# A rewritten opening in a fixed order, and the small products of recurrence and attention issued in larger groups

## The chip, the cores and the metric

One core of a Trainium2 chip runs one decoder layer in one launch. The time is device microseconds of that launch. Matrix products run on TensorE (PE), copies with a scale and functions from a table on ScalarE (ACT), elementwise work on VectorE (DVE), some of it on GpSimd (POOL). Loads are issued from the queue of SyncE (SP), some from POOL's (among them `wdu`, which the first products of the recurrence read, and the positions, `posi`).

## The reference

The sequence has 256 tokens, the model 1024 channels. One projection gives the inputs of two branches, an RWKV-7 recurrence with 8 heads of 64 channels and an attention with 8 heads of 64; each is projected back, gated, and a gated MLP with a short convolution follows.

```python
h = rms_norm(x, norm1_g); proj = h @ w_in            # 1824 + 1536 + 2048 columns
z = z + mu * (shift_right(z) - z)                     # token shift
w_log = -softplus(-(decay_bias + tanh(xw) @ w_decay_up)) - 0.5
a = sigmoid(aaa_bias + xa @ w_aaa_up)
kk = k*k_k / norm(k*k_k);  k = k * (1 + (a - 1) * k_a)
for each token:                                       # state per head 64 x 64
    sa = S @ (-kk_t)
    S  = S * decay_t + sa (x) (kk_t * a_t) + v_t (x) k_t
    y_t = S @ r_t
y_a = (groupnorm(y) + sum(r*k*r_k) * v) * (sigmoid(xg) @ w_gate_up)
y_b = softmax(causal(q k^T / 8)) v                    # q, k normed, partly rotated
x = x + (sigmoid(gate_a) * (y_a @ w_a) + sigmoid(gate_b) * (y_b @ w_b)) @ w_out
u = rms_norm(x, norm2_g) @ w_up                       # halves ua, ub, 2816 columns each
x = x + (gelu(conv3(ua)) * ub) @ w_down
```

With 256 tokens and attention blocks of 256 keys, the choice of blocks leaves each query only its own block, so the attention is plain causal attention.

## The kernel before

**Full products.** The activations stand as a high and a low part (`hh` and `hl`, both in the tile `hx`; `ybh` and `ybl` for the attention's output). Each weight tile is split in the same way: `raw` (512 KB, four buffers) is loaded by SP, its high part `whi` (four buffers) is cast by ACT (L246; three early tiles by DVE), and the remainder `wlo` (three buffers) is taken by DVE (L256). Only when the remainder is done is the next `raw` issued (`load_next`, L234). Three products per tile follow: high by high (L284), low by high (L286) and high by remainder (L289), each 128x128 by 256 columns; for q, k and v of the attention 512 columns (L305, L306, L309). These are the "full products" below. Their sums go to the PSUM pool `acc` (three banks). The small products of the recurrence use the pool `ch` (three banks), those of the attention `at` (two).

**The opening.** x comes in four pieces on SP's queue, then four weight tiles, then ten small parameter loads into `p_100` (L397: shift factors, biases, norm weights), then the fifth weight tile. x is squared and scaled, turned by PE (`xt`, L352), and written as `hx` by ACT (L357) and DVE (L358). DVE also casts the first weight tile, forms its remainder (L256), copies the parameters from PSUM (`late_params`), sets constants (`late_consts`) and computes the angles of the rotation (`rope_tables`). The first three quarters of a projection give `xwa` and `xg`; products on `xwa` (L494) open the recurrence.

**The recurrence** (thread "chain") works on chunks of 64 tokens, four per sequence, eight heads, in products of 64 rows or 64 columns, so on half of the array. In order: `pw` (L494) gives decay and a; `pss` and `prx` (L546) give the norm of k; POOL and DVE write the scaled keys `KB` (POOL's part at L572); `pgr` (L592) multiplies keys by queries inside each chunk, and DVE masks the result into `G` (L595). The 16x16 diagonal blocks of G go through DRAM to `Tb`, where DVE inverts them in 15 steps of two instructions (L612, L614, on `Xb`), and through DRAM again to `X` (L623). `pk`, `pv` and `pz0` prepare the keys, values and right-hand sides. `level()` extends the inverse from 16 to 32 and from 32 to 64 rows (`pp` L704, `px` L714, `py` L720); level(0) serves chunks 0 and 1, level(1), a thread "lv1" of its own, chunks 2 and 3. Then for each chunk `pz` (L772), `pu` (L779), `pS` (L788) and `pyt` (L804, L808); a thread "gn" normalises the results (`pc`, L754).

**The attention** (thread "att") turns q and k (`qkT`), and then takes four blocks (two halves of the tokens, two halves of the heads): scores `ps` (L876), mask, maximum and exponentials (L889) on DVE and ACT, scaling by the sum (four L893), transposes `ppt` (L904), the product with v, `po` (L913), and the split of the output into `ybh` (ACT, L917) and `ybl` (DVE, L918).

**The order.** A thread "bulk" holds the full products: k, r, v of the recurrence, q, k, v of the attention, eight gate products (`gates(1)`, `gates(0)`), and `branch(1)`, the projection of the attention's output, which waits for "att". A loop takes the threads in turn; each yields a cost (PE's time) and a latency after which it may go on:

```python
cost, lat = next(th[1])
now_t += cost
th[2] = now_t + lat * SLACK.get(th[0], 1.0)
```

So what comes out is one order per engine, in which small groups stand between full products. A scheduler places the rest (`tc.issue_after` adds an edge). After the threads come `branch(0)`, the output projection (its result is turned for the MLP, `xt`), and the MLP (L1044, L1047, L1062 to L1064).

Of the kernel before, what the change touches and what calls it, by code (L numbers as in the profile page):

```python
# [11 lines left out]
I32 = mybir.dt.int32  # L12
# [24 lines left out]
def body(tc, x, positions, norm1_g, w_in, rwkv_mu, w_decay_up, decay_bias, w_aaa_up,  # L37
# [5 lines left out]
    with ctx:  # L43
# [6 lines left out]
        HI_ENG = {i: dve for i in (4, 5, 6)}  # L50
# [36 lines left out]

        p0 = t1("p0", (8, 128))
        nc.gpsimd.dma_start(p0, rows(norm1_g, 8))
        x_sb = load_x()  # L90

        ones = cst.tile([128, 512], mybir.dt.bfloat16, name="ones")
        dve.memset(ones, 1.0)

        def keep_warm(n):

            p = acc("idle")
            for _ in range(n):
                pe.matmul(p, ones[:, 0:128], ones, start=True, stop=True)

        keep_warm(8)
        jp = t1("jp", (128, 128), I32)
        pool.iota(jp, pattern=[[1, 128]], base=0, channel_multiplier=-1)
        ident = cst.tile([128, 128], F32, name="ident")
        pool.tensor_scalar(ident, jp, 0.0, None, op0=OP.is_equal)
        eps1 = cst.tile([128, 2], F32, name="eps1")
        dve.memset(eps1[:, 0:1], NORM_EPS)
        dve.memset(eps1[:, 1:2], GN_EPS)
        warm = cst.tile([128, 1], F32, name="warm")
        act.activation(warm, eps1[:, 0:1], AF.Sqrt)  # L110
        jl = t1("jl", (128, 2, 64), I32)
        for q in range(2):
            pool.iota(jl[64 * q:64 * q + 64], pattern=[[0, 2], [1, 64]], base=0,
                      channel_multiplier=-1)
        p1 = t1("p1", (51, 128))
        p1_loads = []
        at = 0
        mu1 = rwkv_mu[0]
        for r, n in ((mu1[0:1792].rearrange("(n c) -> n c", c=128), 14),
                     (mu1[1696:1824].rearrange("(n c) -> n c", c=128), 1),  # L120
                     (rows(decay_bias, 4), 4), (rows(aaa_bias, 4), 4), (rows(k_k, 4), 4),
                     (rows(k_a, 4), 4), (r_k[0].rearrange("h n -> (h n)").rearrange("(n c) -> n c", c=128), 4),
                     (rows(ln_g, 4), 4), (rows(ln_b, 4), 4), (rows(norm2_g, 8), 8)):
            p1_loads.append((p1[at:at + n], r))
            at += n
        assert at == 51
        p2 = t1("p2", (88, 128))

# [8 lines left out]
        def late_consts():  # L137
            dve.tensor_scalar(gmask[:, 0:64], jl[:, 0], 0.0, None, op0=OP.is_gt)
            dve.tensor_scalar(gmask[:, 64:128], jl[:, 1], 0.0, None, op0=OP.is_ge)
            dve.memset(bones, 0.0)  # L140
            for q in range(2):
                dve.memset(bones[64 * q:64 * q + 64, 64 * q:64 * q + 64], 1.0)
            dve.tensor_reduce(rowf, ident.rearrange("p (a b c) -> p a b c", a=4, b=2)[:, :, 1, :],
                              axis=AX.XY, op=OP.add)
            dve.memset(m16, 0.0)
            dve.memset(m32, 0.0)
            for q in range(4):
                o = 32 * (q % 2)
                dve.memset(m16[32 * q:32 * q + 32, o:o + 16], 1.0)
                if q % 2:  # L150
                    dve.memset(m32[32 * q:32 * q + 32, 0:32], 1.0)
            dve.tensor_scalar(m16, m16, rowf, None, op0=OP.mult)
            dve.tensor_scalar(cmask, jp, 0.0, NEG, op0=OP.is_gt, op1=OP.mult)
            dve.memset(rst, 1.0)
            dve.memset(rst.rearrange("p (c i) -> p c i", i=64)[:, :, 0:1], 0.0)

# [3 lines left out]
        pt = atp("pt")  # L160
        pe.transpose(pt[:, 0:8], p0, ident[:8, :8])
        keep_warm(3)
# [21 lines left out]
        def small_loads():  # L184
            nc.gpsimd.dma_start(p2[0:66], conv_w[0].rearrange("w (n c) -> (w n) c", c=128))
            nc.gpsimd.dma_start(p2[66:88], rows(conv_b, 22))

            nc.gpsimd.dma_start(wdu[0:64], w_decay_up[0])
            nc.gpsimd.dma_start(wdu[64:128], w_aaa_up[0])
            nc.gpsimd.dma_start(wgu[:, 0], w_gate_up[0, 0:128])  # L190

            pool.memset(wgu[0:96, 1], 0.0)
            nc.gpsimd.dma_start(wgu[96:128, 1], w_gate_up[0, 128:160])
            for i, g in enumerate((q_norm_g, k_norm_g)):
                nc.gpsimd.dma_start(gqk[:, i], bass.AP(tensor=g.tensor, offset=g.offset,
                                                       ap=[[0, 128], [1, 64]]))
            nc.gpsimd.dma_start(posi, positions[0].rearrange("(t p) -> p t", p=128))

        trig = cst.tile([128, 2, 2, HALF], F32, name="trig")

        def rope_tables():
# [23 lines left out]
            act.activation(trig, ang, AF.Sin)  # L225
# [3 lines left out]
        def load_next():  # L229
            if queue:  # L230
# [3 lines left out]
                nc.sync.dma_start(raw[:, :k * c].rearrange("p (k c) -> p k c", k=k), ap)  # L234
# [4 lines left out]
        def split_hi(eng=None):  # L239
            if raws:  # L240
                eng = eng or HI_ENG.get(nhi[0])
                nhi[0] += 1
                raw, k, c = raws.pop(0)
                hi = wp.tile([128, 1024], F32R, name="whi", tag="whi", bufs=NHI)
                if eng in (None, act):
# [5 lines left out]
        def split_lo():  # L251
            if halves:
# [3 lines left out]
                dve.tensor_tensor(lo[:, :n], raw[:, :n], hi[:, :n].bitcast(F32), op=OP.subtract)  # L256
# [56 lines left out]
        def norm_t(src, g0, tagn, cuts):  # L313
# [40 lines left out]
            def second(mid=lambda a, d: None):  # L354
                for k in range(8):
# [4 lines left out]
                    if k == 3:  # L360
                        mid(a, d)
# [785 lines left out]
```

## Time and profile before

| | us |
|---|---|
| median of 3 runs | 437.18 (437.11 to 437.87) |
| the profiled execution | 437.27 |
| its span in the trace | 435.5 |
| PE busy, share of the span | 424.9, 98% |
| DVE busy | 327.6, 75% |
| ACT busy | 241.9, 56% |
| POOL busy | 12.8, 3% |
| full products with 256 columns: L284, L286, L289 | 64.0 + 62.5 + 40.1 |
| full products with 512 columns: L305, L306, L309 | 20.3 + 18.8 + 15.0 |
| MLP, up: L1044, L1047 | 96.7 + 54.6 |
| MLP, down: L1062 to L1064 | 31.2 each |
| casts of weights on ACT, L246 (121, 1050 ns each) | 126.4 |
| remainders on DVE, L256 (125, 1219 ns each) | 152.0 |

The rows of the trace in the next sections begin with the start in us from the span's start and the busy time in us; then engine, line, operation, what is written from what is read, the shape and the count. A bracket at the end gives the idle time just before the row and what ended it. Matmuls overlap in the array, so the busy times of PE add up to more than passes; the distance from one start to the next tells what a matmul costs. In the page's 40 slices PE is busy for nine tenths or more in all but four (the first two, the seventh and the last), and the granted clock of TensorE is nine tenths or more in all but the second. 70.7 MB move in the span, at 162 GB/s.

### The profile page before, as it was taken

The page shows a single profiled execution, that of the slowest core. Times are in us where ns is not written, and L with a number is a line of the kernel's source. Part 1 is how long each engine was busy: PE and PEld are TensorE (multiplying, and loading weights), DVE is VectorE, ACT ScalarE, POOL GpSimd, SP SyncE. Part 2 cuts the span into 40 slices and gives each one's busy share as a digit, 9 for nine tenths or more (in the row PEclk, how much of TensorE's full clock was granted, in tenths as well). Part 3 has the DMA queues.
Part 4 walks back from the last instruction along what each step waited for, and adds up shares of the span by engine and source line. Part 5 has one row for each costly group of instructions (what it writes and reads, how often), then busy time and mean ns, then how long its engine had stood idle before and what let it go on. Part 6 is the DMA issues. An engine that isn't in the chain of part 4 may idle for free.

```text
span 435.5 us, 8161 instructions
## 1 busy us (share of the span) xinstructions
PE 424.9 (98%) x3248; PEld 367.7 (84%) x3248; DVE 327.6 (75%) x589; ACT 241.9 (56%) x391; POOL 12.8 (3%) x21
## 2 busy tenths in 40 slices
PE   7899998999999999999999999999999999999996
PEld 3789996788899989799997887888888888888885
DVE  4695899698456568676796489797797786786883
ACT  6489852644375446777355377554454564564540
POOL 6000040000000000000000000000000000000000
PEclk9899999999999999999999999999999999999999
DMA  8764836543658331153566365766656556656622
GB/s 232 202 190 124 238 99 195 134 130 52 194 151 233 85 115 53 50 189 116 179 174 192 121 187 161 231 195 197 192 180 208 189 168 211 199 156 212 192 76 96
DMA packets 62187, 70.72 MB, mean 162 GB/s; under 512 B 8898, under 2 KB 52617, under 8 KB 62150
## 3 DMA queue, kind: packets, MB, share of 16 engines
q1 hardware_dynamic: 61750, 69.50, 53.4%
q0 software_dynamic: 400, 0.71, 0.6%
q8 instruction: 25, 0.41, 0.4%
q14 instruction: 12, 0.10, 0.1%
HBM read 68.76 MB, written 1.44 MB: 161 GB/s over the span
## 4 chain that ended last, share of the span: by engine, by line
PE 80%; ACT 6%; DVE 6%; DMA 4%; issue 1%; SPq 1%; DVEq 0%; ACTq 0%
PE acc L1044 17%; PE acc L1047 8%; PE acc L284 6%; PE acc L286 5%; PE acc L289 5%; PE acc L305 4%; PE f L1063 4%; PE f L1062 4%; PE f L1064 4%; PE acc L306 4%; PE acc L309 4%; DMA raw<-in_w_in_dram 3%; DVE wlo L256 2%; ACT whi L246 2%; PE ps L876 1%
## 5 line engine op out<-in xcount | busy, mean ns | idle before, releaser
L246 ACT CAST whi<-raw 128x1024 fp32r<-128x1024 f32 x121 | 126.4, 1050 | 117.5 <-PE acc L1044 46.6
L256 DVE TENSOR_TENSOR wlo<-raw,whi 128x1024 fp32r<-128x1024 f32 x125 | 152.0, 1219 | 45.9 <-PE acc L1047 12.9
L1044 PE MATMUL acc<-hx,whi 128*128 128x512 f32 x352 | 96.7, 395 | 0.6 <-DVE bs L1052 0.6
L1044 PEld LDWEIGHTS acc<-hx,whi 128*128 128x128 f32 x352 | 60.1, 188 | 9.1 <-DVE bs L1052 1.0
L284 PE MATMUL acc<-hx,whi 128*128 128x256 f32 x248 | 64.0, 292 | 0.7 <-ACT whi L246 0.5
L286 PE MATMUL acc<-hx,whi 128*128 128x256 f32 x248 | 62.5, 285 | 0.3 <-DVE hx L358 0.2
L1047 PEld LDWEIGHTS acc<-hx,wlo 128*128 128x128 f32 x352 | 53.4, 188 | 7.9
L1047 PE MATMUL acc<-hx,wlo 128*128 128x256 f32 x352 | 54.6, 278 | 0.0
L284 PEld LDWEIGHTS acc<-hx,whi 128*128 128x128 f32 x248 | 47.4, 191 | 2.9 <-ACT whi L246 0.7
L286 PEld LDWEIGHTS acc<-hx,whi 128*128 128x128 f32 x248 | 47.4, 191 | 1.9 <-DVE hx L358 0.7
L289 PE MATMUL acc<-hx,wlo 128*128 128x256 f32 x248 | 40.1, 285 | 1.0 <-DVE wlo L256 0.9
L289 PEld LDWEIGHTS acc<-hx,wlo 128*128 128x128 f32 x248 | 33.8, 192 | 1.7 <-DVE wlo L256 1.6
L1063 PE MATMUL f<-whi,hb 128*128 128x512 f32 x80 | 31.2, 390 | 0.0
L1064 PE MATMUL f<-wlo,hb 128*128 128x512 f32 x80 | 31.2, 390 | 0.0
L1062 PE MATMUL f<-whi,hb 128*128 128x512 f32 x80 | 31.2, 390 | 0.0
L1052 DVE TENSOR_REDUCE an<-acc 128x256 f32<-128x512 f32 x22 | 15.2, 689 | 7.2 <-PE acc L1047 6.3
L305 PE MATMUL acc<-whi,hx 128*128 128x512 f32 x48 | 20.3, 425 | 0.0
L306 PE MATMUL acc<-whi,hx 128*128 128x512 f32 x48 | 18.8, 392 | 0.0
L1064 PEld LDWEIGHTS f<-wlo,hb 128*128 128x128 f32 x80 | 15.0, 188 | 3.2
L1062 PEld LDWEIGHTS f<-whi,hb 128*128 128x128 f32 x80 | 15.0, 188 | 2.8
L1063 PEld LDWEIGHTS f<-whi,hb 128*128 128x128 f32 x80 | 15.0, 188 | 2.7
L309 PE MATMUL acc<-wlo,hx 128*128 128x512 f32 x48 | 15.0, 393 | 0.0
(280 smaller groups left out, 637.9 us busy)
## 6 DMA issues: line engine op xcount, KB each, us to landing
raw<-in_w_ffn_up_dram SPq DMA_DIRECT2D x44, 512.0 KB
raw<-in_w_in_dram SPq DMA_DIRECT2D x43, 512.0 KB
raw<-in_w_ffn_down_dram SPq DMA_DIRECT2D x22, 512.0 KB
raw<-in_w_out_dram SPq DMA_DIRECT2D x8, 512.0 KB
x<-in_x_dram SPq DMA_DIRECT2D x8, 256.0 KB
raw<-in_w_branch_b_dram SPq DMA_DIRECT2D x4, 512.0 KB
raw<-in_w_branch_a_dram SPq DMA_DIRECT2D x4, 512.0 KB
out_dram<-o SPq DMA_DIRECT2D x3, 256.0 KB
```

Of the source, the lines that this page charges most:

```text
L246: act.copy(hi[:, :k * c], raw[:, :k * c])
L256: dve.tensor_tensor(lo[:, :n], raw[:, :n], hi[:, :n].bitcast(F32), op=OP.subtract)
L284: pe.matmul(om, wh[:, k, ms], xh[:, k0 + k], start=k0 + k + m == 0, stop=False, skip_group_check=True)
L286: pe.matmul(om, wh[:, k, ms], xl[:, k0 + k], start=False, stop=False, skip_group_check=True)
L289: pe.matmul(om, wl[:, k, ms], xh[:, k0 + k], start=False, stop=k0 + k == nk - 1 and m == n - 1, skip_group_check=True)
L305: pe.matmul(ps_[t], xh[:, K, ts], wh[:, k], start=K == 0, stop=False)
L306: pe.matmul(ps_[t], xl[:, K, ts], wh[:, k], start=False, stop=False)
L1044: pe.matmul(ps_[m], wh[:, k, ms], hx[:, k0 + k].rearrange("p a s -> p (a s)"), start=k0 + k == 0, stop=False, skip_group_check=True)
L1047: pe.matmul(ps_[m][:, 0:S], wl[:, k, ms], hh[:, k0 + k], start=False, stop=k0 + k == 7, skip_group_check=True)
L1062: pe.matmul(fin[f], hb[:, 0, i, ts], wh[:, 0, cs], start=st, stop=False)
L1063: pe.matmul(fin[f], hb[:, 1, i, ts], wh[:, 0, cs], start=False, stop=False)
L1064: pe.matmul(fin[f], hb[:, 0, i, ts], wl[:, 0, cs], start=False, stop=False)
```

## The change

It has four parts.

1. **The opening** is written as one function, `first_steps`, under `tc.manual_schedule`: PE, ACT, DVE and POOL issue in the order of the code. The ten parameter loads go from SP to POOL; eleven of POOL's loads stand ahead of its first remainder and eight behind it. The remainder of the first weight tile is formed by POOL (`split_lo(pool)`), not DVE. The first weight tile is loaded in two pieces, norm_g on ACT's queue; the constants are set by POOL; the sums of the first projection are taken for both halves in turn (L413, L417). `rope_tables` moves into the bulk thread.
2. **The recurrence**: the products of a step stand in one group where there were two to four. `pw` is one group on four banks; `pk` comes before `pgr`; `pgr` runs as two groups of 32 products, each on four banks (two of `ch`, two of `at`); `pv` and `pz0` are one group each; the two halves of `level()` are joined (`below`, `masked`, `onto`), and the thread "lv1" is gone. The "gn" thread waits until the thread that ran last was not "bulk" (`joined`). All yields have new numbers, and the factors SLACK are not used.
3. **The attention**: the first half of the tokens is one block of eight heads, the second two of four; the product with v (`weighted`) takes all heads at once; the four scalings by the sum become one instruction.
4. **The order of the bulk**: k, r, q of the attention, v, k of the attention, the first gate, v of the attention; then the attention thread starts, with seven gate products left.

```diff
-        HI_ENG = {i: dve for i in (4, 5, 6)}
+        joined = [False]
...
-        for dst, src in p1_loads:
-            nc.sync.dma_start(dst, src)
...
+        def small_loads(n):
+            for _ in range(n):
+                nc.gpsimd.dma_start(*loads.pop(0))
...
+        def first_steps():
+            for i in range(NRAW):
+                load_next(i == 0)
...
+            nc.scalar.dma_start(p0, rows(norm1_g, 8))
...
+            small_loads(11)
...
+            for k in range(6):
+                high(k)
+            for k in range(2):
+                dve.tensor_copy(hi[:, k * 512:k * 512 + 512], raw[:, k * 512:k * 512 + 512])
+                low(k)
+            split_lo(pool)
+            small_loads(len(loads))
+            split_hi()
+            high(6)
+            high(7)
+            for k in range(2, 8):
+                low(k)
+            split_lo()
+            split_hi()
...
             late_params()
+            split_lo()
+            split_hi()
+            act.activation(warm, eps1[:, 0:1], AF.Sigmoid)
             late_consts()
...
+            for g in range(2):
+                pg = [[p.rearrange("p (u i) -> p u i", u=4) for p in pj] for pj in banks("pgr")]
+                for ct in (2 * g, 2 * g + 1):
...
+                yield 2.1, (5.0, 0.1)[g]
...
-            yield 0, 16.0
-            yield from level(0)
-            threads.insert(1, ["lv1", level(1), 0.0])
+            yield 0, 11.0
+            pp = [below(g) for g in range(2)]
+            P = [masked(pp[g], m16) for g in range(2)]
+            yield 2.5, 3.5
+            adds = [onto(0, P[0], 0), onto(1, P[1], 0), onto(0, P[0], 1)]
+            for a in adds:
+                a()
+            yield 3.3, 4.5
+            pp = [below(g) for g in range(2)]
+            add = onto(1, P[1], 1)
...
-                for h in range(nh):
-                    dve.tensor_scalar(sc[:, h], sc[:, h], sm[:, h:h + 1], None, op0=OP.mult)
-                yield 0, 5.0
+                dve.tensor_tensor(sc, sc, sm[:, :, None].to_broadcast([128, nh, nk]), op=OP.mult)
+                yield 0, 6.0 + 0.8 * nh
...
+            p0 = yield from scores(0, 0, 8)
+            yield weighted(0, p0)
+            pa = yield from scores(1, 0, 4)
+            pb = yield from scores(1, 1, 4)
+            yield weighted(1, pa + pb)
...
-                th[2] = now_t + lat * SLACK.get(th[0], 1.0)
+                th[2] = now_t + lat
+                if cost:
+                    joined[0] = th[0] != "bulk"
```

Three places of the orders, each an unbroken run of rows.

**The opening, POOL.** Before, after x's norm weight and the index tables (the names are the tiles written, and the tensors in DRAM that are read; `p_101` holds the parameters of the convolution):

```order
L113 IOTA jl 64x128
L188 DMA wdu<-in_w_decay_up_dram 64x512
L189 DMA wdu<-in_w_aaa_up_dram 64x512
L185 DMA p_101<-in_ffn_conv_w_dram 66x128
L186 DMA p_101<-in_ffn_conv_b_dram 22x128
L190 DMA wgu<-in_w_gate_up_dram 128x512
L192 MEMSET wgu 96x512
```

and in the change, from the ninth parameter load on (`p_70` is what was `p_100`, `p_71` what was `p_101`):

```order
L180 DMA p_70<-in_rwkv_ln_b_dram 4x128
L180 DMA p_70<-in_norm_g_dram 8x128
L180 DMA p_71<-in_ffn_conv_w_dram 66x128
L243 TENSOR_TENSOR wlo<-raw,whi 128x1024
L180 DMA p_71<-in_ffn_conv_b_dram 22x128
L180 DMA wdu<-in_w_decay_up_dram 64x512
L180 DMA wdu<-in_w_aaa_up_dram 64x512
```

A remainder now stands in POOL's order, with `wdu`, which the first products of the recurrence read, behind it.

**The opening, SP.** Before, the fifth weight tile (the first of the eleven in the last row) stood behind the parameter loads:

```order
L234 DMA raw<-in_w_in_dram 128x4x256
L397 DMA p_100<-in_rwkv_mu_dram 14x128
L397 DMA p_100<-in_rwkv_mu_dram 1x128
L397 DMA p_100<-in_decay_bias_dram 4x128
L397 DMA p_100<-in_aaa_bias_dram 4x128
L397 DMA p_100<-in_rwkv_k_k_dram 4x128
L397 DMA p_100<-in_rwkv_k_a_dram 4x128
L397 DMA p_100<-in_rwkv_r_k_dram 4x128
L397 DMA p_100<-in_rwkv_ln_g_dram 4x128
L397 DMA p_100<-in_rwkv_ln_b_dram 4x128
L397 DMA p_100<-in_norm_g_dram 8x128
L234 DMA raw<-in_w_in_dram 128x4x256 x11
```

In the change SP's queue begins so (the two pieces of 2x256 are one tile):

```order
L81 DMA x<-in_x_dram 128x512 x4
L221 DMA raw<-in_w_in_dram 128x2x256 x2
L221 DMA raw<-in_w_in_dram 128x4x256
L221 DMA raw<-in_w_in_dram 128x8x128
L221 DMA raw<-in_w_in_dram 128x4x256 x8
```

The fourth tile is the first of the last row's eight, and the fifth follows it with nothing between.

**The end of attention, PE.** Before, the steps of the last block of scores (`ppt` turns the probabilities `sc`) stand between gate products, which read `hx`:

```order
L289 MATMUL acc<-hx,wlo 128x256 x4
L772 MATMUL pz<-Sn,AR 64x64 x8
L904 MATMUL ppt<-ident,sc 128x128 x4
L284 MATMUL acc<-hx,whi 128x256
L286 MATMUL acc<-hx,whi 128x256
L284 MATMUL acc<-hx,whi 128x256
L286 MATMUL acc<-hx,whi 128x256
L284 MATMUL acc<-hx,whi 128x256
L286 MATMUL acc<-hx,whi 128x256
L284 MATMUL acc<-hx,whi 128x256
L286 MATMUL acc<-hx,whi 128x256
L289 MATMUL acc<-hx,wlo 128x256 x4
```

In the change the last steps of the recurrence (`pyt`) are followed by the last block's eight `ppt`, all sixteen `po` of the second half of the tokens, and then by the first products of `branch(1)`:

```order
L826 MATMUL pyt<-VU,G_784 64x64
L826 MATMUL pyt<-VU,G_785 64x64
L918 MATMUL ppt<-ident,sc 128x128 x8
L931 MATMUL po<-pT,qkv 64x128 x16
L271 MATMUL acc<-ybh,whi 128x256 x2
L774 MATMUL pc<-ident,yc 64x64 x8
L273 MATMUL acc<-ybl,whi 128x256
```

The last gate products stand ahead of this piece, between the last `ps` and the last `pu`.

More of the change, by code (lines that the diff above doesn't have):

```diff
@@ L392, in body @@
         queue += [wd[:, 20:21, :], wd[:, 21:22, :]]
-        for _ in range(NRAW):
-            load_next()
-        for dst, src in p1_loads:
-            nc.sync.dma_start(dst, src)
-        hh, hl, xn, part, first, turn, second = norm_t(x_sb, G1, "1", (0, 512, 1024))
-        for t in range(2):
-            part(t, 0)
-            part(t, 1)
-            if t:
-                with tc.issue_after(last):
-                    last = dve.tensor_copy(par[:, 0:8], pt[:, 0:8]).ins
-                with tc.issue_after(last):
-                    last = first(t)
-            else:
-                last = first(t)
-            turn(t)
@@ L440, in now @@
                     return e.value
-        with tc.issue_after(mid[0]):
-            p = now(proj2())
         xwa = t1("xwa")
@@ new lines, in masked, with onto @@
+            def masked(p, mk):
+                P = b2("P", [128, 8, 64])
+                dve.tensor_tensor(P, p, mk[:, None, :].to_broadcast([128, 8, 64]), op=OP.mult)
+                return P
+            def onto(g, P, side):
+                p, p4 = bank("px")
+                for u, i in us[g]:
+                    for q in range(2):
+                        l, r = X[bsl(q), 1, u], P[bsl(q), i]
+                        if side:
+                            l, r = r, l
+                        pe.matmul(p[bsl(q), i], l, r, start=True, stop=True)
+                return lambda: dve.tensor_tensor(pair(X[:, side], g), pair(X[:, side], g), p4, op=OP.add)
@@ new lines, in chain @@
+            yield 0, 11.0
[8 more added lines that the diff above has]
+            add = onto(1, P[1], 1)
+            P = [masked(pp[g], m32) for g in range(2)]
+            add()
+            yield 3.3, 4.5
+            for a in [onto(g, P[g], 1) for g in range(2)]:
+                a()
@@ L729, in chain @@
+            yield 2.3, 4.0
             ny = {}
@@ L749, in group_norm @@
                     dve.tensor_tensor(yc, yc, st[:, 2][:, :, None].to_broadcast([128, 4, 64]), op=OP.mult)
-                    yield 0, 1.0
+                    yield 0, 6.0
+                    while not joined[0] and "chain" not in done:
+                        yield 0, 0.1
                     p = chp("pc").rearrange("p (a n) -> p a n", a=8)
@@ L951, in bulk, with attention_input @@
             yield from proj4("r", 0)
-            yield from proj4("v", 8)
-            for i in range(3):
+            def attention_input(i):
                 qkv.append(b4("qkv", (128, 2, 8, 64)))
@@ L958, in bulk @@
                     finish_qk(ps_[t], i, t)
-            threads.insert(1, ["att", attention(), 0.0])
-            yield from gates(1)
-            yield from gates(0)
+            while not last_exp:
+                yield 0, 0.5
+            rope_tables()
+            yield from attention_input(0)
+            yield from proj4("v", 8)
+            yield from attention_input(1)
+            yield from gates(1, 0)
+            yield from attention_input(2)
+            threads.insert(1, ["att", attention(), now_t + 3.0])
+            for j in range(1, 4):
+                yield from gates(1, j)
+            for j in range(4):
+                yield from gates(0, j)
             while "att" not in done:
```

485 lines of the change are left out of this document (228 added, 257 removed).

## The prediction

> **What bounds the kernel now.** I read the page's head first, and the chain that ended last.
>
> ```profile
> span 435.5 us, 8161 instructions
> ...
> PE 80%; ACT 6%; DVE 6%; DMA 4%; issue 1%; SPq 1%; DVEq 0%; ACTq 0%
> ```
>
> TensorE (PE) holds 80% of the chain, so a microsecond counts only if it shortens PE's own stream or a wait inside it. The view of PE's waits has, beside some in the first 20 us that come below, two of note before the FFN:
>
> ```profile
> PE pgr L592 <- DVE G L595: 1.1, 1, 1.1
> ...
> PE acc L284 <- ACT whi L246: 0.5, 1, 0.5
> ```
>
> That is little. What is left sits in the stream itself, and the timeline shows where: products on half of the array (64 rows or columns) stand between full-size ones.
>
> ```profile
> 147.75 0.63 PE L289 MATMUL acc<-hx,wlo 128*128 128x256 f32 x4
> 148.31 1.15 PE L720 MATMUL py<-X,P 64*64 64x64 f32 x32
> 149.39 0.39 PE L284 MATMUL acc<-hx,whi 128*128 128x256 f32 x1
> 149.61 0.28 PE L286 MATMUL acc<-hx,whi 128*128 128x256 f32 x1
> 149.73 0.28 PE L284 MATMUL acc<-hx,whi 128*128 128x256 f32 x1
> ...
> 137.34 1.15 PE L714 MATMUL px<-P,X 64*64 64x64 f32 x32
> 138.32 1.10 PE L720 MATMUL py<-X,P 64*64 64x64 f32 x32
> ```
>
> Matmuls overlap, so I go from start to start, the first column. A full product starts 0.12 after the one before it (149.61 to 149.73). The four ahead of the group take 0.56 instead of 0.48: 0.08 for going in. The first after it takes 0.22 instead of 0.12: 0.10 for coming out. And 32 small products take 1.08 when a full one follows (148.31 to 149.39), but 0.98 when more of their own shape follow (137.34 to 138.32): another 0.10. So **a group costs 0.28 to 0.30 us for its two edges**, whatever is in it; 0.30 is what I use. A group of whole-array transposes costs less; these are the full products behind the eight of prx (L546):
>
> ```profile
> 53.28 0.72 PE L289 MATMUL acc<-hx,wlo 128*128 128x256 f32 x4
> 53.84 0.28 PE L284 MATMUL acc<-hx,whi 128*128 128x256 f32 x1
> ```
>
> Four products take 0.56 here instead of 0.48: 0.08 to 0.09 for such a group.
>
> **Term 1, the groups.** Counted in the two orders of PE, between the first full product and the first transpose of x before the FFN: 49 groups now, 36 of them on half the array; 27 in the change, 20 on half the array. The number of full products between is the same, 1128. 16 x 0.30 + 6 x 0.09 = 5.3 us less. Changes of shape inside groups go from 24 to 19, at about the same 0.10: 0.5 more. **-5.8 us.** Bounds: -7 with 0.36 a group, -1 if the cost only moves inside the merged groups, which the pair at 137.34 speaks against.
>
> **Term 2, PSUM banks.** The 1.1 us wait of pgr for G comes from two groups that share three banks. The change runs them as two larger groups on four banks, with 30 full products (5.5 us at these pitches) between. **-1.2**, bounds 0 and -1.4.
>
> **Term 3, the first 26 us.** Now:
>
> ```profile
> 9.85 0.35 PE L284 MATMUL acc<-hx,whi 128*128 128x256 f32 x1
> ...
> 13.29 0.39 PE L289 MATMUL acc<-hx,wlo 128*128 128x256 f32 x1 [0.74 <-DVE wlo L256]
> ...
> 18.85 0.23 PE L169 MATMUL pt<-ident,p 51*128 51x51 f32 x1 [0.70 <-DMA p<-in_norm_g_dram]
> ...
> 25.71 1.14 PE L494 MATMUL ch<-xwa,wdu 64*128 64x256 f32 x8
> ...
> 17.35 0.29 SPq L397 DMA_DIRECT2D p<-in_norm_g_dram  x1
> 17.76 14.44 SPq L234 DMA_DIRECT2D raw<-in_w_in_dram  x7
> ```
>
> From 9.85 to 25.71 PE runs 85 full products, some 10.0 us of work in 15.9. The fifth weight tile is issued only at 17.76, behind ten parameter loads on SP's queue. The change sends those through POOL, and has run 73 products when its 497 comes; 12 products at 0.117 are 1.4, so what it must beat is 24.3. I work its front out from these rows:
>
> ```profile
> 9.29 2.29 ACT L357 ACTIVATE hx<-xt,par 128x256 fp32r<-128x256 f32 x6 [0.30 <-PE xt L352]
> 9.79 1.66 DVE L358 SCALAR_TENSOR_TENSOR hx<-xt,par,hx 128x256 fp32r<-128x256 f32 x4
> 12.02 1.22 DVE L256 TENSOR_TENSOR wlo<-raw,whi 128x1024 fp32r<-128x1024 f32 x1
> 13.35 1.04 ACT L246 CAST whi<-raw 128x1024 fp32r<-128x1024 f32 x1 [1.77 <-DMA raw<-in_w_in_dram]
> 58.60 3.24 POOL L572 TENSOR_TENSOR KB<-av,L 128x1024 f32<-128x1024 f32 x1 [46.91 <-DVE av L570]
> ```
>
> x arrives as before, so the first product again stands near 9.8. The low halves (DVE, 0.42 each, a half cast of 0.35 between) let sixteen products end by 12.1. The first remainder moves from DVE (1.22) to POOL: from 10.65, at the 3.24 that POOL needs for one operation of this size, to 13.9. PE waits 1.8 there, then runs 8, 16 and 8 products to 17.6, for the second tile's cast is done by 12.7 (six activations, then 1.04) and its remainder by 15.2. POOL's product also holds raw's first buffer, so the fifth tile is issued at 13.9. I give it 3.6 to land, an estimate: 1.9 for 512 KB at the 278 GB/s of the windows row of 10 to 13.5 us below, and 1.5 to 1.8 of latency (the 4 KB of norm_g, issued at 17.35, free PE at 18.85). That is 17.5. DVE's order puts its cast ahead of the parameter copies: these end at 18.9, the third remainder at 20.1, xwa and its tanh at 20.9, and 497 starts there. **-3.4**, bounds 0 (rival 2) and -4.5.
>
> POOL's price is the bold step. [...]
>
> One more wait, of 0.5 for a cast (L246), should go, since ACT loads two tables fewer in that stretch; I count 0.3 for small new waits. **-0.2.**
>
> **Term 4, what the order costs: X.** The block inverse goes through DRAM and comes back as X:
>
> ```profile
> 76.00 1.16 PE L592 MATMUL pgr<-AR,KB 64*128 64x128 f32 x16
> ...
> 90.12 0.16 DVE L612 TENSOR_TENSOR tmp<-Tb,Xb 128x15 f32<-128x15 f32 x1
> 99.56 0.17 DVE L614 TENSOR_TENSOR Xb<-Xb,tmp 128x15 f32<-128x15 f32 x1
> ...
> 103.71 4.03 SPq L623 DMA_DIRECT2D X<-d  x8
> 119.42 0.56 PE L704 MATMUL pp<-X,G 64*64 64x64 f32 x10
> ```
>
> Now X's last load is issued at 107.7 and pp stands at 119.4, 42 after the last pgr. In the change pp comes 36 after it, and DVE's order mixes more into the 30 steps of Xb (two remainders, four bonus products, a whole q/k finish): some 15 us instead of 9.8. Summed, X's first half arrives 0.7 us after pp would start. **+0.7**, bounds 0 and 4.
>
> **Term 5, the end of attention.** Now the last block of scores is covered: gate products stand between each of its steps.
>
> ```profile
> 181.55 1.13 PE L876 MATMUL ps<-qkT,qkT 64*128 64x256 f32 x6
> ...
> 187.38 0.49 ACT L889 ACTIVATE sc<-sc,mx 128x256 f32<-128x256 f32 x1
> 188.22 1.14 DVE L893 TENSOR_SCALAR sc<-sc,sm 128x256 f32<-128x256 f32 x4
> ...
> 189.73 0.66 PE L904 MATMUL ppt<-ident,sc 128*128 128x128 f32 x4
> ...
> 193.87 1.28 ACT L747 ACT_TABLE_LOAD   x1
> 196.70 0.42 DVE L918 TENSOR_TENSOR ybl<-po,ybh 128x256 fp32r<-128x256 f32 x1 [0.53 <-ACT ybh L917]
> ```
>
> From ps to ybl it takes 15.6 us (181.55 to 197.12). In the change PE has only 24 full products and eight small pieces (ps among them) from ps to the first product that reads ybl: about 3.0 + 7.0 = 10.0 us, and no gate is left. **+5.5.** Bounds: 0.5, with the same steps back to back (ps 1.1, adds 0.8, maximum 1.2, four exponentials 2.1, scaling 1.4, transposes, copies and po 2.6, ybl 1.3: 10.5), and 9.8, with two table loads like that at 193.87 (ACT's order has them before the exponentials), a cast and a gate's tanh in the way: 4.2 more. I take the middle since it is before's own.
>
> An idle PE costs more than the idle time. The windows view:
>
> ```profile
> 10.00:13.50 3.50, 2.23 (x9) 1.31 (x10) 3.07 (x6) 1.73 (x6) 0.72 (x1) 1.00 1.12 278
> 13.50:17.00 3.50, 3.50 (x18) 3.50 (x18) 2.20 (x4) 2.56 (x4) 0.00 (x0) 0.51 0.60 169
> ```
>
> After 3.5 us with nine products the granted clock (third column from the end) is 0.51 for the next 3.5. The same after the idle end of attention costs half of what runs slowly: **+1.0**, bounds 0 and 3.4. [...]
>
> **Sum.** -5.8 - 1.2 - 3.4 - 0.2 + 0.7 + 5.5 + 1.0 = -3.4 us. The profiled execution took 437.27 us (435.5 of span and 1.8 around it), the median of the runs is 437.18, so they are the same here. 437.3 - 3.4 = **433.9 us**, with its own range of 431 to 436.5.
>
> **Rivals.**
> 1. *The end is covered after all*: the score chain runs at its 10.5 us, and the clock stays: 433.9 - 5.0 - 1.0 = 427.9. For it: DVE and ACT have less of the bulk's work there. Against it: both have queued work ahead of the steps. Chance 0.18.
> 2. *POOL's loads hold the front.* The row is
>
> ```profile
> 10.96 0.72 POOL L197 DMA_DIRECT2D posi<-in_positions_dram  x1 [2.59 <-DMA wdu<-in_w_decay_up_dram]
> ```
>
> and the view of DMA issues has the time to landing last:
>
> ```profile
> wdu<-in_w_decay_up_dram POOLq DMA_DIRECT2D x1, 128.0 KB, 7.4
> p<-in_norm_g_dram POOLq DMA_DIRECT2D x1, 4.0 KB, 3.6
> ```
>
> POOL's tenth load waited until its second had landed, 7.4 us after that one's issue. The change puts eleven loads ahead of POOL's remainder and eight behind. With 7.4 for each, the remainder starts 1.8 later and wdu lands near 23.8, 2.9 after 497 would start: 436.8. Against it: those first loads are tiny, and norm_g's took 3.6. Chance 0.13.
> 3. *Slower: the end is longer.* At 9.8 of stall and two slow windows (3.4) the end costs 13.2 instead of 6.5: 440.6. It decides from 9.9 us on, which is the sum of all other terms. Chance 0.16.
> 4. *Merging saves nothing*, because shapes inside a group cost as much: 433.9 + 4.8 = 438.7. Chance 0.06.
>
> **How the numbers follow.** The forecast has 0.47. Faster than 437.3 by over 0.2% (0.9 us, about what a measurement of this kernel can tell from no change): the forecast, rival 1 and a little of 2, 0.67. Within it: most of 2, 0.12. Slower: 3, 4 and a rest, 0.21. The range runs from rival 1 to short of rivals 3 and 4: 428 to 438.5.
>
> **What would show it.** Term 1: 27 groups before the FFN, and 0.3 us from their last start to the second full product. Term 2: no wait of pgr for G. Term 3: 497 near 21 us, a wait of about 1.8 for wlo with POOL as releaser, SP's fifth tile near 14. Term 4: a wait of pp for X. Term 5: idle PE between ppt and the first product on ybl, and a granted clock of 0.5 after it. Wrong it would be if the first 30 us are no shorter, or if the end of attention costs under 2 or over 10 us.

## The result, and the profile after

| | before | the change |
|---|---|---|
| median, us | 437.19 (437.11 to 437.87, 4 runs) | 430.79 (430.27 to 431.12, 4 runs) |
| ratio | | 0.9848, 95% interval 0.9836 to 0.986 |
| the profiled execution, its span | 437.27, 435.5 | 431.12, 429.0 |

It is faster by 6.4 us; the prediction's sum was 3.4. The page's head and chain of the changed kernel, and the view of PE's waits (us in total, times, longest):

```profile
span 429.0 us, 8164 instructions
...
PE 89%; ACT 4%; DVE 3%; DMA 2%; issue 1%; POOL 1%; SPq 0%; DVEq 0%; ACTq 0%; POOLq 0%
```

```profile
PE ppt L918 <- DVE sc L909: 1.9, 1, 1.9
...
PE acc L276 <- DVE wlo L243: 1.1, 1, 1.1
PE pc L774 <- DVE yc L767: 0.8, 1, 0.8
PE acc L413 <- DVE hx L386: 0.7, 1, 0.7
PE acc L417 <- POOL wlo L243: 0.7, 1, 0.7
PE acc L271 <- ACT ybh L935: 0.7, 1, 0.7
```

PE's share of the chain rose from 80% to 89%. pgr's wait for G and the wait of 0.5 for a cast are gone, there is none of pp for X, and three waits have come at the end of attention (sc, yc, ybh). To see where the rest went I took all starts of PE's products from the first full product to the first `xt` before the MLP and split them: full products at their own pitch (0.117 us, 0.231 with 512 columns), what they took beyond it (edges of groups, and a halved clock), the small products, and pauses of over 0.25 us. A group is an unbroken run of small products between full ones. The MLP behind this place is the same to 0.1 us in the kernel before and in the change; the other rows are the experiments of the next section.

| kernel | groups | full, 1128 | beyond the pitch | small | pauses | sum |
|---|---|---|---|---|---|---|
| before | 49 | 154.0 | 10.1 | 55.9 | 5.4 | 225.4 |
| the change | 27 | 154.0 | 4.7 | 53.7 | 6.7 | 219.0 |
| old_opening | 27 | 154.0 | 5.7 | 54.7 | 8.0 | 222.3 |
| new_opening | 49 | 154.0 | 9.1 | 56.0 | 5.6 | 224.6 |
| new_opening_sin_later | 47 | 154.0 | 10.5 | 56.2 | 5.0 | 225.7 |
| new_opening_pss_later | 44 | 154.0 | 7.7 | 54.5 | 3.1 | 219.3 |
| six_more_groups | 33 | 154.0 | 6.2 | 54.7 | 5.7 | 220.6 |
| gate_kept | 31 | 154.0 | 5.7 | 52.3 | 3.2 | 215.2 |

Against the terms of the prediction, up to the same place (the opening up to the first product on xwa, with 12 products at 0.117 added since the change has run 73 there and the kernel before 85):

| term | forecast | by the two traces |
|---|---|---|
| 1 groups | -5.8 | -7.6 |
| 2 pgr's wait for G | -1.2 | -1.2 |
| 3 opening | -3.4 | -1.7 |
| 3 wait for a cast | -0.2 | -0.7 |
| 4 X | +0.7 | 0 |
| 5 idle at the end of attention | +5.5 | +3.6 |
| 5 halved clock | +1.0 | about +1.3 |
| sum | -3.4 | -6.3 |

Term 1's figure is not read from a row of its own: it is what remains of the difference between the two traces when the other rows are taken off it, and it rests on the experiments below. The figures of term 3 rest on the front of the changed kernel:

```profile
11.46 2.39 POOL L243 TENSOR_TENSOR wlo<-raw,whi 128x1024 fp32r<-128x1024 f32 x1 [2.06 <-DVE whi L395]
...
13.90 1.20 PE L417 MATMUL acc<-hx,wlo 128*128 128x256 f32 x8 [0.69 <-POOL wlo L243]
...
22.54 0.70 PE L497 MATMUL at<-xwa,wdu 64*128 64x256 f32 x4
```

### The profile page after: what moved, and what is told of

Read it like the earlier page. It is cut to its first block, busy times and chain, and to the rows that moved or that the text cites. A ratio compares the mean times of both kernels' runs of the same rounds, so it can differ in the third digit from the quotient of the medians.

```text
span 429.0 us, 8164 instructions
## 1 busy us (share of the span) xinstructions
PE 416.8 (97%) x3249; PEld 365.9 (85%) x3249; DVE 322.0 (75%) x553; ACT 239.1 (56%) x386; POOL 27.1 (6%) x47
## 4 chain that ended last, share of the span: by engine, by line
PE 89%; ACT 4%; DVE 3%; DMA 2%; issue 1%; POOL 1%; SPq 0%; DVEq 0%; ACTq 0%; POOLq 0%
PE acc L1080 17%; PE acc L1083 8%; PE acc L271 8%; PE acc L276 8%; PE acc L273 8%; PE acc L292 4%; PE acc L293 4%; PE acc L296 4%; PE f L1099 4%; PE f L1098 4%; PE f L1100 4%; PE px L727 1%; DMA x<-in_x_dram 1%; DMA raw<-in_w_ffn_up_dram 1%; PE pp L711 1%; PE pgr L611 1%
## 5 line engine op out<-in xcount | busy, mean ns | idle before, releaser
L1080 PEld LDWEIGHTS acc<-hx,whi 128*128 128x128 f32 x352 | 60.1, 188 | 9.1 <-DVE bs L1088 1.0
L1083 PEld LDWEIGHTS acc<-hx,wlo 128*128 128x128 f32 x352 | 53.4, 188 | 7.9
L271 PE MATMUL acc<-hx,whi 128*128 128x256 f32 x232 | 58.4, 287 | 0.0
L273 PE MATMUL acc<-hx,whi 128*128 128x256 f32 x232 | 56.5, 279 | 0.0
L1083 PE MATMUL acc<-hx,wlo 128*128 128x256 f32 x352 | 54.6, 278 | 0.0
L271 PEld LDWEIGHTS acc<-hx,whi 128*128 128x128 f32 x232 | 43.7, 188 | 1.4 <-issue 0.5
L273 PEld LDWEIGHTS acc<-hx,whi 128*128 128x128 f32 x232 | 43.8, 189 | 0.4 <-issue 0.3
L276 PE MATMUL acc<-hx,wlo 128*128 128x256 f32 x232 | 36.1, 278 | 1.1 <-DVE wlo L243 1.1
L276 PEld LDWEIGHTS acc<-hx,wlo 128*128 128x128 f32 x232 | 30.9, 188 | 1.3 <-DVE wlo L243 1.3
L292 PE MATMUL acc<-whi,hx 128*128 128x512 f32 x48 | 19.3, 402 | 0.0
L293 PE MATMUL acc<-whi,hx 128*128 128x512 f32 x48 | 18.8, 392 | 0.0
```

Of the source, the lines that this page charges most:

```text
L271: pe.matmul(om, wh[:, k, ms], xh[:, k0 + k], start=k0 + k + m == 0, stop=False, skip_group_check=True)
L273: pe.matmul(om, wh[:, k, ms], xl[:, k0 + k], start=False, stop=False, skip_group_check=True)
L276: pe.matmul(om, wl[:, k, ms], xh[:, k0 + k], start=False, stop=k0 + k == nk - 1 and m == n - 1, skip_group_check=True)
L292: pe.matmul(ps_[t], xh[:, K, ts], wh[:, k], start=K == 0, stop=False)
L293: pe.matmul(ps_[t], xl[:, K, ts], wh[:, k], start=False, stop=False)
L1080: pe.matmul(ps_[m], wh[:, k, ms], hx[:, k0 + k].rearrange("p a s -> p (a s)"), start=k0 + k == 0, stop=False, skip_group_check=True)
```

## The experiments

### What a group costs

six_more_groups issues pv and pz0, one group each in the change, as four each:

```diff
                         pe.matmul(pv[c // 2][hs, c % 2, ct], ch4(zv)[hs, ct, c], ident[hs, hs],
                                   start=True, stop=True)
+                if c < 3:
+                    yield 0.62, 0.05
...
-            yield 0, 11.0
+            yield 0, 2.7
```

> The changed kernel, where the one group of pv and the one of pz0 are issued as four each with full products between (6 groups more, the same products; the latency before pp is cut by as much, so that all later groups stand where they stood). If an edge costs 0.30 us, +1.8: 432.6 us. If the whole gain of the 22 groups that went lies in edges, 8.1 / 22 = 0.37 each: +2.2, 433.0 us. If merging itself saved nothing and the gain came from elsewhere (pairs of products that were torn apart, waits), 430.8 to 431.1 us.

Measured: 432.72 us (ratio to before 0.991, 0.9883 to 0.9937). PE's timeline of the change around pv, and the first of the four in the experiment:

```profile
82.33 0.63 PE L296 MATMUL acc<-wlo,hx 128*128 128x512 f32 x2
82.89 2.08 PE L654 MATMUL pv<-ident,zv 64*64 64x64 f32 x64
84.90 0.50 PE L292 MATMUL acc<-whi,hx 128*128 128x512 f32 x1
85.23 0.39 PE L293 MATMUL acc<-whi,hx 128*128 128x512 f32 x1
```

```profile
81.09 0.63 PE L296 MATMUL acc<-wlo,hx 128*128 128x512 f32 x2
81.64 0.68 PE L654 MATMUL pv<-ident,zv 64*64 64x64 f32 x16
82.26 0.50 PE L292 MATMUL acc<-whi,hx 128*128 128x512 f32 x1
82.59 0.39 PE L293 MATMUL acc<-whi,hx 128*128 128x512 f32 x1
```

Start to start: two full products take 0.55 or 0.56 ahead of a group instead of 0.46, the first behind it 0.33 instead of 0.23, and four groups of 16 take 4 x 0.62 = 2.48 where one of 64 took 2.01, 0.16 for each of the three that were added. That is 0.36 for a group. Over the part between the opening and the last scores the experiment needs 2.3 us more, 0.39 for each of six. So the edges are real, and dearer than the 0.30 that I took. (Its own opening was 0.97 us shorter than in the change's profile, see below, so the total shows less than 2.3. By the total alone, 0.30 and 0.37 a group can't be told apart; the rows and the 2.3 us decide it.)

The kernel before also paid for something that I had counted as an edge only: its scores stood as one product and then three. One product reads rows 0 to 63 of the array, the next rows 64 to 127, so this cut separates the two products of a pair. scores_in_pairs cuts each block of scores after two products, scores_one_alone after one (the two edits, each by itself):

```diff
                     for q, hs in PAR:
                         pe.matmul(pq[q][:, i], qT[hs, 2 * j + i, ts], kT[hs, 2 * j + i, 0:nk],
                                   start=True, stop=True)
+                    if i == 0:
+                        yield 0.5, 0.05
...
+                        if i == 0 and q == 0:
+                            yield 0.25, 0.05
```

> The changed kernel with each block of scores cut once between products 2 and 3 (after a pair, one product on rows 0 to 63 and one on rows 64 to 127). Read in the trace, not in the total, since the cut also moves what stands at the end. Theory: products on the two halves of the array run beside each other, so a pair is whole and only an edge is paid. The second half's first block (ps with 256 keys, 1.06 us in one group) should take about 0.6 + 0.6 = 1.2 us as two groups of two.

> The same with the cut after the first product, as the kernel before had it (1 + 3). If a product without its neighbour costs as much as a pair, the block takes 0.62 + 1.06 = 1.7 us, as in the kernel before (0.63 and 1.06), 0.5 more than 2 + 2; if only the cut costs, it takes 1.2 us as well.

One block of 256 keys (two records to a product), in pairs and then with one alone:

```profile
156.75 0.70 PE L893 MATMUL ps<-qkT,qkT 64*128 64x256 f32 x4
157.38 0.39 PE L271 MATMUL acc<-hx,whi 128*128 128x256 f32 x1
...
158.96 0.70 PE L893 MATMUL ps<-qkT,qkT 64*128 64x256 f32 x4
159.59 0.68 PE L798 MATMUL pu<-Z,X 64*64 64x64 f32 x16
```

```profile
156.13 0.70 PE L893 MATMUL ps<-qkT,qkT 64*128 64x256 f32 x2
156.75 0.39 PE L271 MATMUL acc<-hx,whi 128*128 128x256 f32 x1
...
158.33 1.13 PE L893 MATMUL ps<-qkT,qkT 64*128 64x256 f32 x6
159.38 0.68 PE L798 MATMUL pu<-Z,X 64*64 64x64 f32 x16
```

Two pairs take 0.63 + 0.63, one and three take 0.62 + 1.05: a product alone on rows 0 to 63 costs as much as the pair. That is 0.4 a block of 256 keys and, by the same reading, half of it for one of 128; four blocks, 1.3 us. The change itself keeps one such cut: its first block, of 128 keys, stands as one product (at 123.65 us) and seven (at 128.93), which take 0.42 + 1.08, where gate_kept, the next experiment, runs the eight in 1.09. Of this some 0.2 is the separated pair, by the same reading, and so about 1.1 of the 1.3 us was saved. By the 0.62 for one and 0.63 for two, the second product of a pair costs 0.01 us here. The totals (436.99 and 436.38 us, one run each) are not comparable: the cuts moved the gate products ahead, and PE then waited 8.4 and 8.2 us at the end of attention.

### The end of attention

In the change's PE timeline and windows (the third column from the end is the granted clock):

```profile
183.53 0.63 PE L822 MATMUL pyt<-Sn,AR 64*64 64x64 f32 x16
184.92 0.65 PE L774 MATMUL pc<-ident,yc 64*64 64x64 f32 x14 [0.76 <-DVE yc L767]
...
186.01 0.68 PE L826 MATMUL pyt<-VU,G 128*64 128x64 f32 x14
188.57 1.97 PE L918 MATMUL ppt<-ident,sc 128*128 128x128 f32 x8 [1.88 <-DVE sc L909]
190.47 2.52 PE L931 MATMUL po<-pT,qkv 128*64 128x128 f32 x32
193.69 0.50 PE L271 MATMUL acc<-ybh,whi 128*128 128x256 f32 x2 [0.69 <-ACT ybh L935]
```

```profile
178.40:182.00 3.60, 3.60 (x44) 3.15 (x41) 3.46 (x11) 2.01 (x5) 0.00 (x0) 1.00 0.83 260
182.00:186.00 4.00, 3.24 (x60) 2.81 (x58) 3.10 (x6) 3.88 (x9) 0.00 (x0) 1.00 0.32 94
186.00:190.00 4.00, 2.12 (x23) 1.97 (x22) 2.85 (x7) 3.13 (x9) 0.00 (x0) 0.78 0.61 200
190.00:194.70 4.70, 4.01 (x53) 3.26 (x51) 2.10 (x6) 3.60 (x7) 0.00 (x0) 0.82 0.00 0
```

Eight ppt take 1.90 us, start to start, where gate_kept needs 1.02 at a full clock. gate_kept moves the first gate product behind v of the attention, so that one gate product more is left when the attention starts:

```diff
-                     (MOBA0 + CW, CW), (GATE0 + D, 256), (MOBA0 + 2 * CW, CW), (GATE0 + D + 256, 256),
+                     (MOBA0 + CW, CW), (MOBA0 + 2 * CW, CW), (GATE0 + D, 256), (GATE0 + D + 256, 256),
...
-            yield from gates(1, 0)
             yield from attention_input(2)
             threads.insert(1, ["att", attention(), now_t + 3.0])
-            for j in range(1, 4):
+            for j in range(4):
```

> The changed kernel with the first gate product moved behind v of the attention, so that the attention thread starts one product (48 full products) earlier and 72 instead of 24 full products stand between the last scores and the end of attention. If PE's idle time there and the halved clock cost 4.3 + 1.2 us, as the trace reads, up to 5.5 less: 425.3 us. If the wait only moves, to the first scores (which need the rotated k) or to pp (which needs X), 429 to 431 us. If the halved clock there cost nothing, 426.5 us.

Measured: **427.74 us** (427.31 to 428.23; ratio 0.9783, 0.9751 to 0.9815), the fastest kernel of the study together with one that follows.

```profile
169.43 1.13 PE L893 MATMUL ps<-qkT,qkT 64*128 64x256 f32 x8
...
183.69 1.09 PE L918 MATMUL ppt<-ident,sc 128*128 128x128 f32 x8
...
189.44 0.62 PE L271 MATMUL acc<-ybh,whi 128*128 128x256 f32 x3 [0.67 <-ACT ybh L935]
```

```profile
182.00:186.00 4.00, 4.00 (x67) 3.54 (x65) 2.06 (x4) 3.91 (x8) 0.00 (x0) 1.00 0.66 191
186.00:190.00 4.00, 3.33 (x53) 2.83 (x51) 2.62 (x7) 2.71 (x6) 0.00 (x0) 1.00 0.65 206
```

The wait for sc is gone and the clock stays full; the pauses at the end fall from 3.6 to 1.1. The gain is not the 5.5 I had hoped for: four groups more come back (31 instead of 27), some 1.4 us, and ybh is still waited for. The median is 3.05 us lower than the change's. With the 1.4 of the groups that is 4.4, against the 3.6 + 1.3 of the table: so the end of attention cost the change 4 to 5 us of what the groups had won.

### The opening

old_opening and new_opening swap only the opening; new_opening keeps the small groups, the attention and the bulk order of the kernel before. The edit of new_opening against the kernel before, cut to its frame (old_opening takes the same lines out of the change and puts the old ones back):

```diff
-        hh, hl, xn, part, first, turn, second = norm_t(x_sb, G1, "1", (0, 512, 1024))
...
-        small_loads()
...
+        with tc.manual_schedule(engines={E.PE, E.Activation, E.DVE, E.Pool}):
+            p = first_steps()
+        masks()
         rope_tables()
...
-            p = now(proj2())
```

> The changed kernel (430.8 us) with the opening of the kernel before; groups, attention and bulk order stay. If the new opening is worth what the prediction's third term says (3.4), 434.2 us. If it is worth what the two traces show up to the start of the first product on xwa with the same work done (about 1.7), 432.5 us. Rival: the opening's gain is lost again before the recurrence starts, since pss, prx and pk wait on DVE and ACT anyway: 431 us.

> The kernel before (437.2 us) with only the new opening; the small groups, the attention and the order of the bulk stay, and rope_tables stands directly behind the opening. By the prediction's third term 433.8 us; by the traces 435.5 us; if the gain is lost before the recurrence, 437 us.

Measured: 432.83 us (0.9886, 0.9837 to 0.9936) and 438.71 us (1.0032, 1.001 to 1.0055). In the full change the opening is worth 1.8 us by the traces (the rest of old_opening's difference stands at the end of attention, where its clock was lower still, 0.50 from 190 to 194 us and 0.70 from 194 to 198). The totals alone do not show it: the interval of old_opening overlaps that of the change (0.9836 to 0.986). Added alone to the kernel before, the opening gains nothing: by the trace PE reaches the first product on `xwa` 2.2 us earlier with the same work done, and this is lost again behind it. The wait that took its place, and ACT's timeline ahead of it:

```profile
PE acc L269 <- ACT whi L231: 1.6, 1, 1.6
```

```profile
31.20 1.28 ACT L515 ACT_TABLE_LOAD   x1
...
33.59 1.28 ACT L208 ACT_TABLE_LOAD   x1
...
35.13 1.28 ACT L516 ACT_TABLE_LOAD   x1
...
38.73 1.03 ACT L231 CAST whi<-raw 128x1024 fp32r<-128x1024 f32 x1
```

A Sin (L208) stands between two Exps (L515, L516), each of the three with a table load of 1.28 us, and a cast stands behind all three loads. In the trace of the change, where the Sin comes behind the second Exp, that Exp (31.26 us) has none. new_opening_sin_later takes one part of the change more, rope_tables in the bulk thread and the Sin behind the second Exp; new_opening_pss_later besides this changes the one number ahead of `pss`:

```diff
-            act.activation(trig, ang, AF.Sin)
+            with tc.issue_after(last_exp[0]):
+                act.activation(trig, ang, AF.Sin)
...
-        rope_tables()
...
             yield from proj4("r", 0)
+            while not last_exp:
+                yield 0, 0.5
+            rope_tables()
```

```diff
-            yield 0, 1.5
+            yield 0, 2.65
             p = chp("pss")
```

> new_opening (438.7 us) with one part of the change more: rope_tables in the bulk thread behind r, and its Sin on ACT only behind the second Exp. Theory: the opening's gain was lost at 38 us, where a cast of a weight tile stood behind three table loads of 1.28 us on ACT (Exp, Sin, Exp again) and PE waited 1.6 us. With the Sin later the wait goes and the gain stays: 1.6 to 2.2 less, 436.5 to 437 us on that run's scale, and about 435.3 by the trace. Rival: another wait on ACT takes its place before the keys, and the time stays at 438 us.

> new_opening_sin_later with one number more: the latency ahead of pss 2.65 instead of 1.5 (times the thread's factor 1.7, so 4.5 us as in the change), which puts 24 full products more ahead of pss and makes it one group of eight. Theory: there PE waited three times for the squares of ACT (0.3 to 0.5 each), and the granted clock fell to 0.51 for the next 3.5 us, which cost the two us that the opening had gained. With pss later neither happens and the gain stays: span 433.4 (435.8 without), 435.5 us against 437.5 for the kernel before. Rival: the wait moves to prx or to the keys, and the span stays above 435.

Measured: 438.06 us (1.0004, 0.9979 to 1.003) and **431.59 us** (0.9861, 0.9838 to 0.9883). The first was a miss: the cast's wait went, but PE then paused at pss for ACT's squares (the view of waits has two such pauses, 0.7 together, where the expectation counted three), and the two windows from 39.5 us read, in this kernel and then with pss later:

```profile
39.50:43.00 3.50, 2.83 (x25) 2.55 (x23) 2.82 (x5) 3.48 (x6) 0.00 (x0) 1.00 0.89 264
43.00:46.50 3.50, 3.50 (x19) 3.50 (x19) 2.34 (x3) 2.84 (x5) 0.00 (x0) 0.51 0.58 155
```

```profile
39.50:43.00 3.50, 3.50 (x34) 3.50 (x32) 2.85 (x5) 3.48 (x7) 0.00 (x0) 1.00 0.79 211
43.00:46.50 3.50, 3.50 (x33) 3.50 (x32) 3.47 (x4) 3.47 (x5) 0.00 (x0) 1.00 0.79 234
```

After two pauses of 0.3 and 0.4 us around the tiny products of pss the granted clock was 0.51 for 3.5 us. Other executions bear this out: of the ten of new_opening_sin_later, the two with a mean granted clock of 1.000 took 435.89 and 435.95 us, 1.6 less than the kernel before, and the four at 0.990 to 0.992 took 438.96 to 439.85 (the four at 0.996 took 435.81 to 438.19). With pss 24 products later neither the pauses nor the halved clock come, and what I had not expected: all of the change's gain but 0.8 us is there, with 44 groups and the old attention. By the table its pauses fall by 1.9 against new_opening_sin_later, the time beyond the pitch by 2.8 (1.6 of it the halved clock), and the small products by 1.7, since the later phase also keeps the first two blocks of scores whole and pgr's G in time. So, by the two tables, the change's large groups won 7.6 and lost 4.9 at the end of attention, and about the same net can be had without most of them.

rst_early, remainder_on_dve and change_again go after 0.9 us: the opening took 12.7 us in the change's profile, 11.8 in those of six_more_groups and gate_kept. DVE's cast of the fifth tile and POOL's first memset, in the change, in gate_kept and in change_again:

```profile
18.26 1.55 DVE L235 CAST whi<-raw 128x1024 fp32r<-128x1024 f32 x1 [2.56 <-PE pt L148]
...
18.28 0.98 POOL L118 MEMSET rst<- 128x1024 bf16 x1
```

```profile
18.16 0.70 DVE L235 CAST whi<-raw 128x1024 fp32r<-128x1024 f32 x1 [2.47 <-PE pt L148]
...
18.28 1.45 POOL L118 MEMSET rst<- 128x1024 bf16 x1
```

```profile
18.04 1.28 DVE L235 CAST whi<-raw 128x1024 fp32r<-128x1024 f32 x1 [2.83 <-DMA raw<-in_w_in_dram]
...
17.79 0.98 POOL L118 MEMSET rst<- 128x1024 bf16 x1
```

change_again is the changed kernel, unaltered. rst_early moves two memsets ahead of POOL's loads, and remainder_on_dve gives the first remainder to DVE:

```diff
         def late_consts():
-            pool.memset(rst, 1.0)
-            pool.memset(rst.rearrange("p (c i) -> p c i", i=64)[:, :, 0:1], 0.0)
...
+            pool.memset(rst, 1.0)
+            pool.memset(rst.rearrange("p (c i) -> p c i", i=64)[:, :, 0:1], 0.0)
             small_loads(11)
```

```diff
-            split_lo(pool)
+            split_lo()
```

> The changed kernel, unchanged, beside the two others on the same chip: 430.8 us. The cast on DVE at 18.2 us takes 0.70 where it begins before POOL's memset of rst and about 1.5 where it begins behind it or just with it.

> The changed kernel with POOL's two memsets of rst (0.98 and 0.61 us in the profile of the changed kernel) ahead of its eleven loads instead of behind the last load. Theory: in that profile the cast on DVE that began at 18.26 took 1.55 us because POOL's memset, which began at 18.28, held what both need; in two other executions the cast began 0.12 to 0.14 before the memset and took 0.70. Then the cast takes 0.7 here always, the product on xwa starts at 21.4 (22.5 in that profile), and the time is 430.3 us, never 431.1. Rival: the cast's time has another cause (its source landing late), and both values show here too.

> The changed kernel with the first remainder on DVE again, not POOL, in its place of the opening. Theory of the change's order: DVE's six low halves behind it come 1.2 us later, PE waits for them instead of 0.7 for POOL's remainder, so the product on xwa is 0.3 to 0.5 later: 431.2 us. [...]

change_again gave 431.13 us (429.82 to 431.82): the cast that began 0.25 behind the memset took 1.28. In these rows the one that came first kept its own length (0.70 for the cast, 0.98 for the memset), and the other was longer by about what was left of it; in the change, where the starts lie 0.02 apart, it was the memset that kept its length. rst_early (430.73 us, 0.9849, 0.9811 to 0.9886) was a miss: the cast now met the next memset, that of wgu (18.54), took 1.12, and xwa's product began at 22.5 as before; the collision moved and was not removed. remainder_on_dve gave 431.96 us (430.38 to 434.19) beside 431.13; the intervals overlap (0.9831 to 0.9912 and 0.9824 to 0.9867), so which engine is better for the remainder stays open. In its trace the opening was 0.7 shorter than in the change's first trace, but its first product began 0.65 later, behind a wait for x's norm.

gate_kept_opening_mended joins gate_kept with rst_early's edit, an earlier third remainder and the fifth cast on ACT; beside the edits shown:

```diff
-                eng = dve if nhi[0] in (4, 5, 6) else act
+                eng = dve if nhi[0] in (5, 6) else act
...
-            late_params()
             split_lo()
+            late_params()
```

> gate_kept (427.7 us) with rst_early's edit, the third remainder ahead of the parameter copies on DVE, and the fifth tile's cast on ACT. Theory: PE's waits for the third wlo go, the product on xwa no longer waits for the cast: 1 to 1.5 less, 426.5 us. Rival: PE then waits in the same place for the parameter copies and xwa: 427.5 us.

Measured: 427.74 us (426.89 to 428.12), the same as gate_kept. PE's wait for the third wlo (0.2 in gate_kept) went, but POOL's remainder, now behind the two memsets, cost 1.2 instead of 0.7, and a wait of 0.6 for ACT's cast came at 35 us. The time is the rival's; the waits are not the ones that it named.

## Why the prediction was right in direction and wrong in size

- **What bounds the kernel**: right. What shortened PE's stream or a wait inside it counted (gate_kept, pss_later), and three edits that moved work among the other engines (rst_early, remainder_on_dve, gate_kept_opening_mended) left the time where it was, within the spread of the runs.
- **Term 1, the step that failed.** "16 x 0.30 + 6 x 0.09" had the count right (27 groups) and the price low: 0.36 to 0.39 for a group on half the array, as six_more_groups shows. I read the edges from few rows, which have 0.08 for the way in where six_more_groups has 0.09 or 0.10, and took 0.10 for the last small product, where six_more_groups has 0.16. And it left out the scores that stood as one and three: about 1.1 us by the pair of experiments. 16 x 0.37 + 6 x 0.09 + 1.1 = 7.6 stands against 7.6; so good an agreement is in part chance, since that 7.6 is a remainder and the prediction's 0.5 for shapes inside groups was not tested. Term 1 came out 1.8 lower than forecast. It is not alone: term 5 is 1.6 lower, X and the cast's wait 1.2 together, while the opening gained 1.7 less than forecast and hid that much of the miss. That the sum is off by no more than 3 us is luck in that respect.
- **Term 2**: right, 1.2 us and no wait left. pss_later has no such wait either, without the four banks, so they were not the only way to it.
- **Term 3**: the wait for POOL's remainder came. The remainder ended near 13.9 and SP issued the fifth tile at 13.88, as worked out (13.9), but by luck: it began at 11.46 instead of 10.65, behind DVE's second half cast, and took 2.39 us instead of 3.24, about twice DVE's 1.22. PE waited only 0.7 instead of 1.8 because its sixteen products ahead, delayed by a wait of 0.7 for `hx`, ended near 13.2 instead of 12.1. What I missed is DVE's cast of 1.55 beside POOL's memset, and that PE then waits 1.1 for the third remainder: the first product on `xwa` stands at 22.5 instead of 20.9. Without the collision, in six_more_groups and gate_kept, it is 21.4 and 21.6. The wait for a cast: 0.7 gone, against 0.2.
- **Term 4**: X's last load was issued at 114.1 and landed 2.3 us later, 0.8 ahead of pp: no wait. DVE took 12.0 us for the 30 steps of Xb, not 15.
- **Term 5**: from ps to ybl 15.95 us, against 15.6 forecast. But PE's own work there took 12.7 of the 16.3 (1.3 of it by the low clock), not 10.0, so 3.6 stayed idle. The halved clock came for some 3.4 us, as 0.78 of 4.0 us and 0.82 of 4.7 us work out, and cost 1.3 against 1.0. The longest pause ahead of it was 1.9 us; in the prediction's own row PE was busy for 2.23 of the 3.5 us ahead of the clock of 0.51.
- **The rivals**: the first (end covered, 427.9) did not happen in the change but is what gate_kept built, at 427.7; that the two numbers meet is chance, since gate_kept starts from other sizes of all terms and has four groups more. The second did not happen: POOL's remainder waited for DVE's cast, not for a load, and the first product on `xwa` followed the full products ahead of it without a wait for `wdu`. The third and fourth are refuted by 3.6 us of idle time and by six_more_groups.

What stays open: whether the change's gain with a covered end and the small groups' phase (gate_kept with pss_later's few edits) would add up, and the remainder's better engine.

## What to carry to other kernels

Count what stands between full products, not only the products: here a group on half the array cost 0.36 to 0.39 us at its two edges (six_more_groups), and a half-array product that was torn from its neighbour 0.62 us, as much as a whole pair (0.63, scores_one_alone and scores_in_pairs). Before merging, look at what the merged steps leave uncovered at the end of their chain, and keep one independent product (here a gate, 48 full products) back for it. And test a new opening together with the latencies behind it: alone it gave all of its gain to the next wait (1.6 us, new_opening), and with that wait gone, to a granted clock of 0.51 for 3.5 us (new_opening_sin_later).

## What the runs showed of the hardware that was not expected

- A cast on DVE (0.70 us by itself) and a memset on POOL (0.98) held each other up: the cast took 1.55 and 1.28 when the memset came with it or first, and the memset 1.45 when the cast came first. One two-input operation of 128x1024 on POOL took 2.39 us (the remainder), another 3.24 (KB, before) and 5.50 us (KB, in the change); why KB takes longer was not tested.
- Two pauses of 0.3 and 0.4 us around a few tiny products were followed by a granted clock of 0.51 for 3.5 us (new_opening_sin_later). It is no rule for pauses as such: in new_opening PE was busy for only 1.94 of 3.5 us, with one pause of 1.6, and the clock stayed full there and in the window behind it. What decides stays open; the tiny products and the place of the pauses were not varied apart.

```profile
37.50:41.00 3.50, 1.94 (x15) 1.55 (x13) 1.69 (x3) 3.50 (x7) 0.00 (x0) 1.00 0.01 3
41.00:44.50 3.50, 3.26 (x27) 3.08 (x27) 3.47 (x6) 3.50 (x8) 0.00 (x0) 1.00 0.60 156
```
